# Routing's small products between the last output columns, idle products beside the gather, and gathered rows turned by a diagonal of their scales

## The chip, the cores and the metric

The kernel runs on one core of a Trainium2 chip. The metric is the time of one execution on the device in microseconds; the median of three runs is given with the lowest and the highest. The profile is of one further execution.

## What is computed

Two blocks in a row, in float32, on 512 tokens of 1024 channels. The first block mixes five groups of channels (short convolution, spatial gating, pooling, Conformer convolution, attention to a memory), with a layer norm. The second has two layers, an mLSTM with a SwiGLU and an HGRN2 mixer with a mixture of eight experts, of which each token takes two; a final root-mean-square norm ends it. The change lies in the mixture of experts:

```python
def moe_swiglu(h, router_w, wg, wu, wd):
    t = h.reshape(bsz * s, d)                       # 512 tokens x 1024
    logits = (t @ router_w).astype(jnp.float32)     # 8 experts
    top_logits, top_idx = lax.top_k(logits, TOP_K)  # 2 of 8
    top_w = jax.nn.softmax(top_logits, axis=-1)
    gates = jnp.einsum('tk,tke->te', top_w, jax.nn.one_hot(top_idx, N_EXPERTS))
    for e in range(N_EXPERTS):                      # hidden width 1408
        y = y + gates[:, e:e + 1] * swiglu(t, wg[e], wu[e], wd[e])
```

`h` is `rmsnorm(x) * (1 + scale) + shift`, so an expert's input row is a row of `x` times a scale of its own (the inverse root mean square), times a vector `A` of channels, plus a vector `B` of channels.

## The kernel before, in words

Activations are kept transposed: channels on the 128 partitions, tokens along the free dimension, so `x[0]` to `x[7]` are 128 x 512 each. A product in float32 accuracy is made of three faster ones (`mm3`, `emm`, type fp32r): each operand is split into a high part, copied by ACT, and a low part, the rest, subtracted by DVE. Weights come through `wload` (L238): SP starts a DMA of 128 x 1024 numbers into `raw`, ACT copies `hi`, DVE subtracts `lo`. Small products (routing, rows, bands) are plain float32 ones.

The Tile framework's scheduler sets the order of each engine from priorities that follow the order of the code; `tc.issue_after(i)` puts what stands in its block behind instruction `i`, and `tc.high_priority()` ahead.

**Routing.** The HGRN2 mixer's output projection makes the eight columns of `x`: columns 0 to 3 together (`cols4`), 4 to 7 one by one (`col`, 24 products of 512 columns each). After each, `post(j)` (L1437) adds the residual (`p_h`), and PE makes that column's part of the router logits (`ra`, four products of 8 columns), and of the mean squares (`mean_squares`, after columns 6 and 7). The rows of `x` times `A` also go to DRAM as tokens x channels (`hnd`): `scaled_rows` multiplies four 128 x 128 blocks by diagonals `dg` (tiles named `f` for the first 512 channels and `q` for the last), `to_dram` copies the bank on ACT and starts the DMA. Rows of the first four columns are made after column 3, those of the last four after column 7 and the inverse root `rs`. From the logits DVE ranks the experts (`selb` is the choice), counts the tokens of each and gives each token its place; `dispatch` (one-hot `OH` against `pay`, on PE) turns that into lists of rows `ii` and scales `sc`.

**The rows of an expert.** `fetch` (L1562) has POOL gather an expert's rows from `hnd` by an indirect DMA and then multiplies them by `sc`: for the first expert half on ACT and half on DVE (`now`), for the other seven on POOL (L1573). An expert has places for 192, 128, 192, 128, 160, 128, 160 and 128 rows in the order of the work: a tile of 128 rows, or one of 128 and one of 64 or 32. `inputs` (L1640) turns the rows back into channels x rows: per half of the channels and tile four transposes into one bank, then four ACT copies that add the bias `B` (high part `eh` or `ex`) and four DVE operations for the low part:

```python
nc.tensor.transpose(ps[:, w * k:w * k + w], xg[:, z:z + 128], ident[0:w, 0:w])
pa = act(eh[:, 4 * m + k, o:o + w], ps[:, w * k:w * k + w], AF.Identity, bias=B[:, 4 * m + k:4 * m + k + 1])
pd = stt(el[:, 4 * m + k, o:o + w], ps[:, w * k:w * k + w], B[:, 4 * m + k:4 * m + k + 1],
         eh[:, 4 * m + k, o:o + w].bitcast(F), OP.add, OP.subtract)
```

**An expert** (L1766) makes gate and up products (`hidden_cols` for two tiles, `hidden_rows` for one), then the down products in two halves of 512 channels (`j`), and scatters its rows with addition to `yd` in DRAM by POOL. `then` prepares and fetches the next expert's rows early in the hidden products, and `inputs` of the next expert is written after the first half of the down products. The last expert's rows are added in SBUF (`combine`, L1824), where ACT also squares the sums for the final norm, each column in a scratch buffer of its own, and `final` scales and stores the result. While the first expert starts, ACT's queue also starts the DMAs that prime `yd` (`beside`).

Of the kernel before, what the change touches and what calls it, by code (L numbers as in the profile page):

```python
# [17 lines left out]
T = 512  # L18
NT = 4
# [158 lines left out]
def tile_kernel(ctx, tc, I, out, dbg=None, upto=99):  # L178
# [42 lines left out]
    def mm(o, l, r, start=True, stop=True):  # L221
        nc.tensor.matmul(o, l, r, start=start, stop=stop)  # L222
# [5 lines left out]
    def mm3(o, wh, wl, xh, xl, first, last):  # L228
        mm(o, wh, xh, first, False)
        mm(o, wh, xl, False, False)  # L230
        mm(o, wl, xh, False, last)
# [4 lines left out]
    fast = {"raw": None, "i": 0}  # L236
# [23 lines left out]
    def col(src, xh, xl, post, j, halves=False):  # L260
# [3 lines left out]
        for k0 in range(0, K, 8):  # L264
            m = min(8, K - k0)
            hi, lo = wload(src[:, 128 * k0:128 * (k0 + m)], 128 * m)
            for h in range(2 if halves else 1):
                for r in range(m):
# [4 lines left out]
                    else:  # L273
                        mm3(ps, hi[:, z], lo[:, z], xh[k], xl[k], k == 0, k == K - 1)
# [95 lines left out]
    idle = M(384)  # L370
    for i in range(3):
        mm(idle, O1024, onesk.rearrange("p a b -> p (a b)"))
# [835 lines left out]
    with ExitStack() as st:  # L1208
# [193 lines left out]
        def row_of(v, n, o, bank=M):  # L1402

            ps = bank()
            for k in range(4):
                mm(ps[:, 128 * k:128 * k + 128], v[:, 4 * n + k:4 * n + k + 1].to_broadcast([128, 128]), ident)
            act(o, ps, AF.Copy)

# [14 lines left out]
        def mean_squares(a, last):  # L1423
            for t in range(NT):
                mm(lgm[:, 32 + t:33 + t], ssq[a][:, 128 * t:128 * t + 128], O1024[:, 0:1], False, last and t == 3)
# [10 lines left out]

        def post(j, ps):  # L1437
# [15 lines left out]
        with tc.issue_after(rsqrt(rs[:, 0:4], lgm[:, 32:36], EPS, rs[:, 4:8])):  # L1453
            for t in range(NT):
                to_dram(1, t, scaled_rows(1, t, G()))
# [15 lines left out]
        ts(selb, rk, 2.0, op0=OP.is_lt)  # L1471
# [10 lines left out]
        nc.vector.tensor_copy(out=r8[0], in_=rs[:, None, 0:4].to_broadcast([128, 8, NT]))  # L1482
        parts(pay[..., 2:5], *r8)
# [72 lines left out]

        def tile_of(pays, n0, n, OH, real):
            ps = dispatch(pays, n0, n, OH)
            ii, fi, sc = slots(n, ps, real)
            return n, weights(n, ps), ii, fi, row(n), sc  # L1560

        def fetch(tiles, now=False):  # L1562
# [4 lines left out]
            for t_ in tiles:  # L1567
                r, sc = t_[4], t_[5]
# [24 lines left out]
        fetch(cur, True)  # L1593
# [28 lines left out]
        for n in range(2):  # L1622
            row_of(mods[:, 1, 5, :], n, g2[n], G)
# [5 lines left out]
    with ExitStack() as st:  # L1629
# [10 lines left out]
        def inputs(tiles):  # L1640
# [9 lines left out]
            for m in range(2):  # L1650
                o = 0
                for t_ in tiles:
                    w, xg = t_[0], t_[4]
                    ps = M(4 * w)
                    for k in range(4):
# [9 lines left out]
                pins.append((pa, pd))  # L1665
# [293 lines left out]
```

## Time and profile before

| | us |
|---|---|
| median of three runs (lowest, highest) | 1756.07 (1749.74, 1757.24) |
| profiled execution, its own time | 1755.59 |
| its span in the profile | 1753.8 |
| PE busy | 1702.9 (97%) |
| DVE busy | 1247.8 (71%) |
| ACT busy | 857.6 (49%) |
| POOL busy | 78.1 (4%) |

The profiled execution lasts 1.8 us longer than the span between its first and last recorded work. PE is the engine that is nearly always busy; the mixture of experts runs from about 1201 us, where the last output column ends, to the end. An engine's row in a window gives its busy time, and in brackets the instructions that start there. In a timeline the first number is the start, the second the busy time of the instructions that the row groups (their count stands behind the x); the distance to the next start is what a row of matmuls costs PE, since their ends overlap. What stands in square brackets is idle time ahead of the row and what ended it.

### The profile page before, as it was taken

The page shows a single profiled execution, that of the slowest core. Times are in us where ns is not written, and L with a number is a line of the kernel's source. Part 1 is how long each engine was busy: PE and PEld are TensorE (multiplying, and loading weights), DVE is VectorE, ACT ScalarE, POOL GpSimd, SP SyncE. Part 2 cuts the span into 40 slices and gives each one's busy share as a digit, 9 for nine tenths or more (in the row PEclk, how much of TensorE's full clock was granted, in tenths as well). Part 3 has the DMA queues.
Part 4 walks back from the last instruction along what each step waited for, and adds up shares of the span by engine and source line. Part 5 has one row for each costly group of instructions (what it writes and reads, how often), then busy time and mean ns, then how long its engine had stood idle before and what let it go on. Part 6 is the DMA issues. An engine that isn't in the chain of part 4 may idle for free. (4 is left out here: it accounts for less than half of the span.)

```text
span 1753.8 us, 25198 instructions
## 1 busy us (share of the span) xinstructions
PE 1702.9 (97%) x8987; PEld 1426.5 (81%) x8987; DVE 1247.8 (71%) x2215; ACT 857.6 (49%) x1431; POOL 78.1 (4%) x90
## 2 busy tenths in 40 slices
PE   9999998999999999999999999999999999999995
PEld 7867787787788888888878888787987987978975
DVE  7887888857666766443255766655889889889887
ACT  5535346755443222232243222444667667767675
POOL 1000001000000000000010000000001102011000
PEclk9999998999999999999999999999999999999998
DMA  8434731344426777433342111104879789889885
GB/s 273 138 114 143 228 122 50 108 159 153 154 86 210 241 244 242 140 96 91 105 127 84 58 52 61 61 25 152 311 242 373 248 251 364 266 266 343 263 290 202
DMA packets 96474, 313.02 MB, mean 178 GB/s; under 512 B 10644, under 2 KB 13972, under 8 KB 96344
## 3 DMA queue, kind: packets, MB, share of 16 engines
q1 hardware_dynamic: 90760, 295.88, 50.4%
q0 software_dynamic: 3280, 11.27, 2.8%
q10 hardware_dynamic: 2304, 4.20, 0.6%
q8 instruction: 73, 1.20, 0.3%
q14 instruction: 57, 0.47, 0.1%
HBM read 298.99 MB, written 12.32 MB: 178 GB/s over the span
## 5 line engine op out<-in xcount | busy, mean ns | idle before, releaser
L208 ACT ACTIVATE hi<-raw 128x1024 fp32r<-128x1024 f32 (+3 forms) x473 | 475.5, 1008 | 543.4 <-PE g L222 439.3
L219 DVE TENSOR_TENSOR lo<-raw,hi 128x1024 fp32r<-128x1024 f32 (+3 forms) x473 | 547.7, 1169 | 254.0 <-ACT hi L208 246.0
L222 PE MATMUL g<-xh,hi 128*128 128x512 f32 (+1 forms) x912 | 356.4, 393 | 5.0 <-ACT xh L208 5.0
L222 PE MATMUL g<-xl,hi 128*128 128x512 f32 (+1 forms) x912 | 358.1, 393 | 1.3 <-DVE xl L211 1.2
L222 PE MATMUL g<-xh,lo 128*128 128x512 f32 (+1 forms) x912 | 357.7, 393 | 0.0
L222 PEld LDWEIGHTS g<-xh,hi 128*128 128x128 f32 x912 | 173.5, 191 | 41.5 <-ACT xh L208 5.9
L222 PEld LDWEIGHTS g<-xl,hi 128*128 128x128 f32 x912 | 174.3, 191 | 36.8 <-DVE xl L211 2.8
L222 PEld LDWEIGHTS g<-xh,lo 128*128 128x128 f32 x912 | 174.4, 191 | 33.6 <-issue 1.1
L222 PE MATMUL g<-ex,hi 128*128 128x384 f32 (+1 forms) x704 | 197.1, 359 | 4.3 <-DVE ex L211 4.3
L222 PE MATMUL g<-ex,lo 128*128 128x192 f32 (+1 forms) x704 | 173.7, 247 | 1.7 <-DVE lo L219 1.6
L222 PE MATMUL g<-hi,th 128*128 128x512 f32 (+2 forms) x462 | 148.3, 384 | 0.3 <-ACT th L208 0.2
L388 DVE SCALAR_TENSOR_TENSOR ar<-ar,one,crow 128x1024 f32<-128x1024 f32 x96 | 122.0, 1283 | 24.7 <-DMA ar<-in_ada_dram 22.3
L222 PEld LDWEIGHTS g<-ex,lo 128*128 128x128 f32 x704 | 137.2, 195 | 2.7 <-DVE lo L219 2.6
L222 PEld LDWEIGHTS g<-ex,hi 128*128 128x128 f32 x704 | 135.0, 192 | 5.0 <-DVE ex L211 4.8
L222 PE MATMUL g<-hi,eh 128*128 128x512 f32 (+1 forms) x384 | 112.9, 373 | 0.0
L222 PE MATMUL g<-lo,th 128*128 128x512 f32 (+2 forms) x275 | 104.9, 382 | 0.0
L222 PEld LDWEIGHTS g<-hi,th 128*128 128x128 f32 (+1 forms) x462 | 83.1, 183 | 19.7 <-ACT th L208 1.3
L222 PEld LDWEIGHTS g<-hi,eh 128*128 128x128 f32 x384 | 70.8, 188 | 10.1
L222 PE MATMUL g<-lo,eh 128*128 128x512 f32 (+1 forms) x192 | 71.8, 374 | 4.0 <-DVE lo L219 4.0
L222 PE MATMUL g<-fh,hi 128*128 128x512 f32 (+1 forms) x198 | 73.1, 369 | 0.0
L222 PE MATMUL g<-fl,hi 128*128 128x512 f32 (+1 forms) x198 | 72.7, 367 | 0.0
L222 PE MATMUL g<-fh,lo 128*128 128x512 f32 (+1 forms) x198 | 72.7, 367 | 0.0
(473 smaller groups left out, 2516.3 us busy)
## 6 DMA issues: line engine op xcount, KB each, us to landing
ar<-in_ada_dram SPq DMA_DIRECT2D x96, 512.0 KB, 4.4
raw<-in_e_w_dram SPq DMA_DIRECT2D x88, 512.0 KB, 5.1
raw<-in_e_d_dram SPq DMA_DIRECT2D x79, 512.0 KB, 4.9
raw<-in_e_a_dram SPq DMA_DIRECT2D x64, 512.0 KB, 4.7
raw<-in_f_gu_dram SPq DMA_DIRECT2D x44, 512.0 KB, 3.6
raw<-in_e_b_dram SPq DMA_DIRECT2D x32, 384.0 KB, 7.5
raw<-in_w_in_dram SPq DMA_DIRECT2D x22, 512.0 KB, 3.5
raw<-in_f_d_dram SPq DMA_DIRECT2D x16, 512.0 KB, 3.5
```

The lines of the kernel that those rows point to most:

```text
L208: return nc.scalar.activation(out=o, in_=i, func=f, **kw).ins
L219: return nc.vector.tensor_tensor(out=o, in0=a, in1=b, op=op).ins
L222: nc.tensor.matmul(o, l, r, start=start, stop=stop)
L388: nc.vector.scalar_tensor_tensor(out=raw, in0=raw, scalar=pace["one"], in1=crow, op0=OP.mult, op1=OP.mult, accum_out=mods[:, l, i, j:j + 1])
```

## The change

Five things are changed.

1. Logits and rows of finished columns are issued behind later columns: after column 4 the logits of columns 0 and 1 and the first half's rows of token blocks 0 and 1, after column 5 those of 2 and 3, after column 6 the logits of 4, 5 and 6 and the row products of columns 4 and 5 (`later_rows`), which stay in four banks; those of columns 6 and 7 come after the last logits and the last mean squares.
2. The parts of `rs` for the payload (`r8`) are issued after the choice.
3. Four idle float32 products of 384 columns follow the products of `g2`, beside the gather.
4. Gathered rows are no longer multiplied by their scales. DVE makes a diagonal of an expert's scales (`diagonal`), and `inputs` multiplies: one float32 product of the identity with `B`, spread over the bank, and per block of channels the rows with the diagonal, added to it. One ACT copy and one DVE subtraction follow per half and tile. `inputs` is now a generator, of which a piece is issued after each weight load of the second down half.
5. All squares of `combine` use one scratch buffer (`l4`).

```diff
+        def logits(j):
+            for t in range(NT):
+                i = mm(lgm[:, 8 * t:8 * t + 8], x[j][:, 128 * t:128 * t + 128], ra[:, 8 * j:8 * j + 8], False, False)
+            return i
+        def later_rows(k):
+            if not late_rows:
+                late_rows.extend([M(), M(), M(), G()])
+            for t in range(NT):
+                mm(late_rows[t][:, 128 * k:128 * k + 128], x[4 + k][:, 128 * t:128 * t + 128], dg[4 + k])
         def post(j, ps):
             p_h(j, ps)
-            for t in range(NT):
-                mm(lgm[:, 8 * t:8 * t + 8], x[j][:, 128 * t:128 * t + 128], ra[:, 8 * j:8 * j + 8], False, False)
+            at = fast["mm"]
+            with tc.issue_after(at):
+                for i in {4: (0, 1), 5: (2, 3), 6: (4, 5, 6)}.get(j, ()):
+                    logits(i)
+            for t in {4: (0, 1), 5: (2, 3)}.get(j, ()):
+                with tc.issue_after(at):
+                    ps = scaled_rows(0, t, M())
+                to_dram(0, t, ps)
             if j == 6:
                 mean_squares("a", False)
+                with tc.issue_after(at):
+                    later_rows(0)
+                    later_rows(1)
             if j == 7:
-                mean_squares("b", True)
-            if j == 3:
-                for t in range(NT):
-                    to_dram(0, t, scaled_rows(0, t, M()))
+                with tc.issue_after(logits(7)):
+                    later_rows(2)
+                with tc.issue_after(mean_squares("b", True)):
+                    later_rows(3)
...
+        def diagonal(n0, n, sc):
...
+                diag["t"] = hp.tile([128, T], F, tag=("l5", "l6")[diag["i"]], name="dgs")
+            d = diag["t"][0:n, n0:n0 + n]
+            ts(d, ident[0:n, 0:n], sc[:, 0:1])
+            return d
...
-                if now:
-                    act(r[:, 0:512], r[:, 0:512], AF.Copy, scale=sc[:, 0:1])
-                    ts(r[:, 512:1024], r[:, 512:1024], sc[:, 0:1])
-                else:
-                    nc.gpsimd.tensor_tensor(out=r, in0=r, in1=sc[:, 0:1].to_broadcast([t_[0], D]), op=OP.mult)
...
-            row_of(mods[:, 1, 5, :], n, g2[n], G)
+            i = row_of(mods[:, 1, 5, :], n, g2[n], G)
+        idle_mms(4, i)
...
+                    mm(p3, ident, B[:, ks, None].to_broadcast([128, 4, w]), True, False)
                     for k in range(4):
                         z = 512 * m + 128 * k
-                        nc.tensor.transpose(ps[:, w * k:w * k + w], xg[:, z:z + 128], ident[0:w, 0:w])
-                    for k in range(4):
-                        pa = act(eh[:, 4 * m + k, o:o + w], ps[:, w * k:w * k + w], AF.Identity,
-                                 bias=B[:, 4 * m + k:4 * m + k + 1])
-                    for k in range(4):
-                        pd = stt(el[:, 4 * m + k, o:o + w], ps[:, w * k:w * k + w], B[:, 4 * m + k:4 * m + k + 1],
-                                 eh[:, 4 * m + k, o:o + w].bitcast(F), OP.add, OP.subtract)
+                        mm(p3[:, k], xg[:, z:z + 128], d, False, k == 3)
+                    pa = act(eh[:, ks, o:o + w], p3, AF.Copy)
+                    pd = tt(el[:, ks, o:o + w], p3, eh[:, ks, o:o + w].bitcast(F), OP.subtract)
...
                     hi, lo = wload(src, w * kn)
+                    if j == 1 and ahead is not None:
+                        xn_ = next(ahead, xn_)
...
-                act(hw(f"l{4 + j}")[:, 0:w], a, AF.Square, accum=fz[:, j, t:t + 1])
+                act(hw("l4")[:, 0:w], a, AF.Square, accum=fz[:, j, t:t + 1])
```

How the order of instructions moves, at three places. First, PE behind column 6, whose last product is the first row (`x_1841` to `x_1843` are the columns 4 to 6, `ra` logits, `q` row products, `onesk` mean squares, `yh` and `yl` the parts of column 7's operand):

```order
 L222 MATMUL g<-yh_7468,lo 128x512
+L222 MATMUL m<-ra,x_1841 128x8 x4
+L222 MATMUL m<-ra,x_1842 128x8 x4
+L222 MATMUL m<-q,x_1841 128x128 x3
+L222 MATMUL g<-q,x_1841 128x128
+L222 MATMUL m<-ra,x_1843 128x8 x4
+L222 MATMUL m<-q,x_1842 128x128 x3
+L222 MATMUL g<-q,x_1842 128x128
 L222 MATMUL g<-yh_7461,hi 128x512
+L222 MATMUL m<-onesk,ssq 128x1 x4
 L222 MATMUL g<-yl_7469,hi 128x512
 L222 MATMUL g<-yh_7461,lo 128x512
```

Twelve products of logits and eight of rows now stand between columns 6 and 7. Before, those logits stood inside columns 5, 6 and 7, the four mean squares in the middle of column 7, and the row products behind it.

Second, PE at the end of the first expert's down products, where a one-tile expert's rows are turned (`row` gathered rows, `dgs` the diagonal, `mods` the bias, `cst` the identity, `th` the hidden activations). Before:

```order
L222 MATMUL g<-hi,th 128x512 x2
L222 MATMUL g<-lo,th 128x512
L1657 MATMUL m<-cst,row 128x128 x8
L222 MATMUL g<-hi,th 128x512
L222 MATMUL g<-lo,th 128x512
```

and now:

```order
L222 MATMUL m<-mods,cst 128x512
L222 MATMUL m<-dgs,row 128x128 x4
L222 MATMUL g<-hi,th 128x512
L222 MATMUL g<-lo,th 128x512
L222 MATMUL g<-hi,th 128x512 x2
L222 MATMUL g<-lo,th 128x512
L222 MATMUL g<-hi,th 128x512
L222 MATMUL g<-lo,th 128x512
L222 MATMUL g<-hi,th 128x512 x2
L222 MATMUL g<-lo,th 128x512
L222 MATMUL m<-mods,cst 128x512
L222 MATMUL m<-dgs,row 128x128 x4
```

The eight transposes in one place become ten products in two places, five to each, with down products between.

Third, DVE before a two-tile expert begins (`ex` its inputs' low part, `lo` low parts of weights, `row` the expert's rows that are scattered). Before:

```order
L211 SCALAR_TENSOR_TENSOR ex<-m,mods,ex 128x64 x3
L211 SCALAR_TENSOR_TENSOR ex<-m,mods,ex 128x128
L219 TENSOR_TENSOR lo<-raw,hi 128x1024
L211 SCALAR_TENSOR_TENSOR ex<-m,mods,ex 128x128
L219 TENSOR_TENSOR lo<-raw,hi 128x1024 x3
L211 SCALAR_TENSOR_TENSOR ex<-m,mods,ex 128x128 x2
L211 SCALAR_TENSOR_TENSOR ex<-m,mods,ex 128x64 x4
L211 SCALAR_TENSOR_TENSOR row<-g,iw,g_9863 128x512
L211 SCALAR_TENSOR_TENSOR row<-g,iw,g_9864 128x512
```

and now:

```order
L219 TENSOR_TENSOR ex<-m,ex 128x4x128
L219 TENSOR_TENSOR lo<-raw,hi 128x1024
L219 TENSOR_TENSOR ex<-m,ex 128x4x64
L219 TENSOR_TENSOR lo<-raw,hi 128x512
L219 TENSOR_TENSOR ex<-m,ex 128x4x128
L219 TENSOR_TENSOR lo<-raw,hi 128x1024
L219 TENSOR_TENSOR ex<-m,ex 128x4x64
L219 TENSOR_TENSOR lo<-raw,hi 128x1024
L211 SCALAR_TENSOR_TENSOR row<-g,iw,g_9863 128x512
L219 TENSOR_TENSOR lo<-raw,hi 128x1024 x2
```

The last seven small operations stood behind the weights' subtractions and directly ahead of the rows; now the fourth and last `ex` has three weights' subtractions and a row behind it before the next expert's own work.

## Rows read from the trace of the kernel before

**Rows 1.** The page, part 1: busy time, share of the span, instructions of each engine.

```profile
PE 1702.9 (97%) x8987; PEld 1426.5 (81%) x8987; DVE 1247.8 (71%) x2215; ACT 857.6 (49%) x1431; POOL 78.1 (4%) x90
```

**Rows 2.** Windows: us, busy of PE, PEld, DVE, ACT, POOL (count), clock, DMA share, GB/s.

```profile
1201.09:1221.61 20.52, 17.16 (x146) 14.75 (x145) 15.41 (x82) 12.69 (x29) 2.08 (x2) 0.93 0.58 178
1221.61:1246.00 24.39, 22.67 (x146) 21.67 (x145) 18.70 (x43) 17.01 (x34) 3.95 (x2) 0.92 1.02 397
1246.00:1715.00 469.00, 459.79 (x2649) 407.42 (x2649) 408.72 (x647) 329.66 (x533) 50.84 (x29) 0.99 0.87 289
1488.30:1491.70 3.40, 3.40 (x16) 3.40 (x16) 3.40 (x13) 2.57 (x5) 2.53 (x2) 0.50 0.88 240
1715.00:1753.80 38.80, 21.08 (x128) 18.41 (x127) 27.02 (x47) 19.53 (x47) 0.00 (x0) 0.79 0.52 182
1218.64:1225.47 6.83, 6.21 (x30) 5.25 (x31) 4.97 (x18) 5.64 (x19) 0.00 (x0) 0.50 1.01 387
```

**Rows 3.** Timeline, transposes of a 128-row tile: start, busy us, engine, line, op, count.

```profile
1288.56 1.03 PE L1657 MATMUL m<-cst,row 128*128 128x128 f32 x8
1289.35 0.48 PE L222 MATMUL g<-hi,th 128*128 128x512 f32 x1
```

**Rows 4.** PE's timeline, float32 products of 512 and of 128 columns, and what follows.

```profile
1134.09 1.02 PE L222 MATMUL g<-k,onesk 128*128 128x512 f32 x2
1134.94 0.49 PE L1338 MATMUL m<-cst,k 128*128 128x128 f32 x3
1204.36 2.25 PE L222 MATMUL g<-q,x 128*128 128x128 f32 x18
1206.45 0.60 PE L1619 MATMUL g<-cst,x 128*128 128x128 f32 x4
```

**Rows 5.** PE's timeline, float32 products of eight columns, and what follows them.

```profile
1202.20 0.96 PE L222 MATMUL m<-ra,x 128*128 128x8 f32 x8
1203.02 0.69 PE L222 MATMUL g<-q,x 128*128 128x128 f32 x4
```

**Rows 6.** PE's waits from 1246 to 1715 (total, times, longest), then PE's timeline.

```profile
PE g L222 <- DVE ex L211: 4.3, 3, 1.5
PE g L222 <- DVE lo L219: 4.0, 3, 1.3
PE m L1759 <- DVE eh L219: 0.8, 3, 0.3
...
1331.17 0.35 PE L222 MATMUL g<-lo,eh 128*128 128x384 f32 x1
1331.35 0.52 PE L222 MATMUL g<-hi,eh 128*128 128x384 f32 x2
1333.19 0.44 PE L222 MATMUL g<-lo,eh 128*128 128x384 f32 x1 [1.32 <-DVE lo L219]
1486.85 0.41 PE L222 MATMUL g<-ex,hi 128*128 128x320 f32 x1 [1.51 <-DVE ex L211]
```

**Rows 7.** Timeline, POOL and DVE: scaling of rows, one DVE operation beside it and alone.

```profile
1322.85 0.27 DVE L215 TENSOR_SCALAR OH<-cst,P1r 128x128 bf16<-128x128 f32 x1
1329.91 2.27 POOL L1573 TENSOR_TENSOR row<-row,sc 64x1024 f32<-64x1024 f32 x1 [0.30 <-DMA row<-hnd,ii]
1330.36 1.91 DVE L215 TENSOR_SCALAR OH<-cst,P1r 128x128 bf16<-128x128 f32 x1
```

**Rows 8.** PE's timeline after column 3: the last row products and the next column.

```profile
1171.46 4.25 PE L222 MATMUL m<-f,x 128*128 128x128 f32 x24
1175.47 0.47 PE L222 MATMUL g<-yh,hi 128*128 128x512 f32 x1
```

**Rows 9.** Timeline, first expert: ACT on the second gather's rows, PE's longest wait.

```profile
1218.40 0.72 ACT L208 ACTIVATE row<-row,sc 64x512 f32<-64x512 f32 x1 [0.77 <-DMA row<-hnd,ii]
1242.01 0.36 PE L222 MATMUL g<-ex,lo 128*128 128x192 f32 x1 [1.25 <-DVE lo L219]
```

**Rows 10.** PE's timeline of the tail, the records that wait longest.

```profile
1736.94 1.66 PE L222 MATMUL m<-el,eh 128*128 128x256 f32 x8 [2.29 <-ACT el L208]
```

More of the change, by code (lines that the diff above doesn't have):

```diff
@@ L221, in mm, with idle_mms @@
     def mm(o, l, r, start=True, stop=True):
-        nc.tensor.matmul(o, l, r, start=start, stop=stop)
+        return nc.tensor.matmul(o, l, r, start=start, stop=stop).ins
+    def idle_mms(n, after=None):
+        with ExitStack() as order:
+            if after is not None:
+                order.enter_context(tc.issue_after(after))
+            ps = M(384)
+            for i in range(n):
+                mm(ps, O1024, onesk.rearrange("p a b -> p (a b)"))
     def split(hi, lo, src):
@@ L230, in mm3 @@
         mm(o, wh, xl, False, False)
-        mm(o, wl, xh, False, last)
+        return mm(o, wl, xh, False, last)
     def log_exp_tables():
         return tc.keep_in_program_order(nc.scalar.preload_act_table_set("natural_log_exp_and_others")).ins
-    fast = {"raw": None, "i": 0}
+    fast = {"raw": None, "i": 0, "mm": None}
     def wload(src, n, after=()):
@@ L368, in tile_kernel @@
     O256, O1024, O128 = onesk[:, 0, :], onesk[:, 1, :], onesk[:, 2, :]
-    idle = M(384)
-    for i in range(3):
-        mm(idle, O1024, onesk.rearrange("p a b -> p (a b)"))
+    idle_mms(3)
     pairsel = const.tile([8, 4, 128], F, name="pairsel")
@@ L1424, in mean_squares @@
             for t in range(NT):
-                mm(lgm[:, 32 + t:33 + t], ssq[a][:, 128 * t:128 * t + 128], O1024[:, 0:1], False, last and t == 3)
+                i = mm(lgm[:, 32 + t:33 + t], ssq[a][:, 128 * t:128 * t + 128], O1024[:, 0:1], False, last and t == 3)
+            return i
         def scaled_rows(n, t, ps):
@@ L1454, in tile_kernel @@
             for t in range(NT):
-                to_dram(1, t, scaled_rows(1, t, G()))
+                to_dram(1, t, late_rows[t])
         L = SM("L", 32)
@@ L1470, in tile_kernel @@
         nc.vector.reduce_sum(out=rk.rearrange("p (t e) -> p t e", e=8), in_=c4, axis=AX.X)
-        ts(selb, rk, 2.0, op0=OP.is_lt)
+        chosen = ts(selb, rk, 2.0, op0=OP.is_lt)
         ts(sel, rk, 2.0, op0=OP.is_lt)
@@ L1481, in tile_kernel @@
         r8 = [lp.tile([128, 8, NT], F, name=f"r8{i}") for i in range(2)]
-        nc.vector.tensor_copy(out=r8[0], in_=rs[:, None, 0:4].to_broadcast([128, 8, NT]))
-        parts(pay[..., 2:5], *r8)
+        with tc.issue_after(chosen):
+            nc.vector.tensor_copy(out=r8[0], in_=rs[:, None, 0:4].to_broadcast([128, 8, NT]))
+            parts(pay[..., 2:5], *r8)
         pp, pc = M(32), M(8)
@@ L1555, in weights @@
             return iw
+        diag = {"i": 0}
+        def diagonal(n0, n, sc):
+            if n0 == 0:
+                diag["i"] = 1 - diag["i"]
+                diag["t"] = hp.tile([128, T], F, tag=("l5", "l6")[diag["i"]], name="dgs")
+            d = diag["t"][0:n, n0:n0 + n]
+            ts(d, ident[0:n, 0:n], sc[:, 0:1])
+            return d
         def tile_of(pays, n0, n, OH, real):
@@ L1559, in tile_of, with fetch @@
             ii, fi, sc = slots(n, ps, real)
-            return n, weights(n, ps), ii, fi, row(n), sc
-        def fetch(tiles, now=False):
+            return n, weights(n, ps), ii, fi, row(n), diagonal(n0, n, sc)
+        def fetch(tiles):
             for t_ in tiles:
@@ L1592, in tile_kernel @@
             cur.append([n, None, ii, fi, row(n), sc])
-        fetch(cur, True)
+        fetch(cur)
+        for c, n0 in zip(cur, (0, 128)):
+            c[5] = diagonal(n0, c[0], c[5])
         with tc.issue_after(last[0]):
@@ L1769, in expert @@
             else:
-                xs, pins = inputs(tiles)
+                xs, pins = list(inputs(tiles))[-1]
             ns = [t_[0] for t_ in tiles]
-            after = []
+            after, ahead, xn_ = [], None, None
             def then():
@@ L1800, in expert @@
                 if j == 0 and after:
-                    after.append(inputs(after[0]))
+                    ahead = inputs(after[0])
                 for i, n in enumerate(ns):
@@ L1816, in expert @@
                         in_=yts[i], in_offset=None, compute_op=OP.add)
+            if after:
+                after.append(xn_)
             return after
@@ L1932, in tile_kernel @@
             x_ = [tile_of(xpay, 0, 128, places(xP, 128), True)]
-            fetch(x_, True)
+            fetch(x_)
             expert(e, x_, combine)
```

22 lines of the change are left out of this document (14 added, 8 removed).

## The prediction

> **What bounds it now.** I read the page's busy shares first. TensorE (PE) is busy 97% of the span, VectorE (DVE) 71%, ScalarE (ACT) 49% and GpSimd (POOL) 4% [rows 1]. So a microsecond that the change adds to PE's work is paid in full unless PE waited there anyway, and one that it takes off POOL or ACT pays only where PE waited for them. The windows then divide the part that the change touches [rows 2]. In the routing (1201.09 to 1221.61) PE works 17.16 of 20.52 us, and part of that is filler. In the first expert's start (1221.61 to 1246.00) it works 22.67 of 24.39 us while the DMA share is 1.02. In the seven further experts (1246 to 1715) it works 459.79 of 469.00 us at a granted clock of 0.99: all that can be won there is 9.2 us of waiting and the spells at 1.2 GHz. The tail (1715 to 1753.80) is 21.08 us of PE in 38.80.
>
> **Turning the rows, after the first expert.** Now eight transposes turn a 128-row tile, and PE gives them 0.79 us (1288.56 to 1289.35) [rows 3]; I charge a narrow tile the same. The change takes them out and puts in, for each half of a tile, one float32 product that spreads the bias over the bank and four that multiply 128 columns of rows by the diagonal. Every float32 product of the trace leaves two records. Two records of 512 columns took 0.85 us from one start to the next; eighteen records of 128 columns took 2.09 us (1204.36 to 1206.45), 0.116 each [rows 4]; narrow ones took 0.103 (0.82 for eight) [rows 5]. For 256 and 128 columns of bias I scale 0.85 to 0.43 and 0.21.
> - A one-tile expert: 2 x (0.85 + 8 x 0.116) = 3.56 less 0.79, +2.8. Four of them: +11.1.
> - A tile of 128 and one of 64: 2 x (0.85 + 0.43 + 0.93 + 0.82) = 6.06 less 1.58, +4.5. One such expert after the first.
> - A tile of 128 and one of 32: 2 x (0.85 + 0.21 + 0.93 + 0.82) = 5.62 less 1.58, +4.0. Two: +8.1.
>
> Together **+23.7 us**, all on PE, which has no room for it: it sits in the stream of the second down half, a piece per weight load. The lower end is the transposes' own spacing, 0.098 per record: 112 records of 128 columns would cost 2.0 less. The upper end is the price taken: the q products have the same shape and ran back to back. The Trainium skill ("TensorE: Matmul & The Clock Gate", Back-to-back issue gap) gives about 81 ns per matmul of 128 columns in a sustained stream; worked out from that page, an estimate, those 112 records would cost 3.9 us less. Row 1204.36 disagrees and decides.
>
> **What goes away there.** The waits of PE that the trace lists are 4.3 us for the last low parts of the next expert's inputs (three times, up to 1.5) and 4.0 us for low halves of weights (three times, up to 1.3) [rows 6]. With a third row they make 9.1 us, nine waits. Each hides some 0.17 us more in the record ahead of it: the two products at 1331.35 and the one at 1333.19 start 1.84 us apart, where two such products take 0.35 (starts at 1331.17 and 1331.35 are 0.18 apart), so 1.49 is lost and 1.32 booked. That makes 10.6 us. The causes:
> - A POOL multiplication of rows by their scales runs 2.27 us, and a DVE operation beside it that takes 0.27 elsewhere took 1.91 [rows 7]. The weights' subtraction behind it came late, and it is the one that 1333.19 waits for; I read the other two waits for weights as of the same kind. All ten POOL multiplications go.
> - At a two-tile handover DVE makes 16 small subtractions, and PE waits at the first product of the next expert. Now one per half and tile, four in all, stand among the weights' subtractions: in DVE's new order the last is followed by a weights' subtraction, a row and two more before anything of the next expert.
>
> After two of these three waits the clock fell: behind the one at 1486.85 it was 0.50 from 1488.30 to 1491.70 [rows 2, 6], and a second spell of 3.4 us like it makes up the 0.99 of the stretch (3.4 x 0.5 x 2 is 0.7% of 469). Half of 3.4 us, twice: 3.4. In all **-14.0 us**. The ends: nothing comes back of the 4.5 us and 3.4 (rival D), or all of it does.
>
> What is late next: PE's own stream. The new ACT copies (one for four) and DVE subtractions are fewer and lie beside it. The ten diagonals on DVE are each one tensor-scalar operation of 128 columns like the 0.27 row, some 2.7 us in all, spread over seven experts with DVE at 408.72 of 469 us: I cost them at nothing; without that cover each is 0.27.
>
> **Routing's small products.** The rows of the first four columns and their logits stood as one cluster after column 3; its last 24 records of 128 columns took 4.01 us (1171.46 to 1175.47), 0.167 each against 0.116, since the clock was low there [rows 8]. Divided among columns 4 and 5, they cost 1.2 us less if it holds. Against this, sixteen q records now run between columns 6 and 7 that before filled PE's time behind column 7, +1.9. The end of column 7 comes about 0.6 later; if the new cluster behind column 6 made a spell of its own, 1.7 more. After it the mean squares stand behind eight records of rows, not four: +0.46. The parts of the scales, issued after the choice, take work out of DVE's chain ahead of the gather that nobody there waits for; I take nothing, 0.3 either way.
>
> **The first expert's inputs.** ACT and DVE scale the rows of the second gather at 1218.40, as they land, and the first product starts at 1221.61, 3.21 us behind [rows 2, 9]. Without the scaling, PE owes after that landing the narrow tile's first four products and both tiles' second half, 0.82 + (0.85 + 0.93) + (0.43 + 0.82) = 3.85 us at 2.4 GHz (+0.6), or twice that at 1.2 GHz (+4.5). The clock was at 0.50 from 1218.64 to 1225.47 [rows 2], after PE had waited; the products from 1221.61 on lost half of 3.86 us by it, 1.9. So the ends are -1.3 (the four idle products hold the clock) and +4.5 (they don't). I take 0.0: they cover the wait for the first landing, not that for the second. The idle products themselves run in that wait; without it they would cost 4 x 0.64 us, 384 columns at the 512-column price. POOL's multiplication in this stage goes too, and with it most of the 1.25 us that PE waited at 1242.01 [rows 9]: -1.1. Stage: 0.6 + 0.46 + 0.0 - 1.1 = **0.0**, from -2.4 to +4.
>
> **The tail.** Records of the last column's sums wait 2.29 us for a part that ACT splits behind squares of the column before [rows 10]. With one scratch buffer for all squares ACT's order changes and that part stands ahead of the second column's squares; DVE's last row operations remain. I take **-0.8**, between -1.5 and +1 (a square that waits for its buffer).
>
> **Sum:** +23.7 - 14.0 + 0.0 - 0.8 = +8.9 on the profiled execution's 1755.59, so **1764.5**. The median of the runs is 0.48 above that execution, less than the sum is good for, and I leave it out. Half a per cent, 8.8 us, is what a measurement of this kernel can tell from no change: the forecast lies on that line.
>
> **Rivals.**
> - **B, cheaper products and a held clock, 1759.** Records at 0.098 (-2.0), the first stage at its best (-2.4), the tail at its best (-0.7). For it: each end has a row. Against: the q records.
> - **C, one pass, 1745 (the other side).** If a float32 product against a diagonal or the identity took one record like the transposes, a one-tile expert would add 2 x (0.43 + 4 x 0.098) - 0.79 = +0.85, the 192 one +1.24, the 160 ones +1.06: +6.8 for +23.7. That gives 1747.6, and with B's stage and tail 1744.5. It decides from one record per product. For it: the transposes, whose data are float32 too, have one. Against: the bands of q and k are plain float32 products and have two each.
> - **D, the handovers stay late, 1772.** The subtractions are fewer, but each now needs a bias product and four more on PE first, and the pieces come one per weight load. If the last DVE subtraction of a two-tile handover ends after PE's last down product, the three waits (4.5 us) and the spells (3.4) remain: 1764.5 + 7.9 = 1772.4. For it: three of three such handovers waited. Against: the new order of DVE. On the spells the rows say that they come after the waits: a granted clock of 0.99 over seven handovers with transposes [rows 2] leaves room for the two seen. The Trainium skill (same page, Part 4: PE-mode transpose) says that transposes don't count as work for the clock in the same way; by it products would hold the clock whatever the waits do, and D would be 3.4 less, 1769. The five handovers with transposes and no spell speak against that, so it gets 0.03 of D's chance.
> - That the change doesn't do what it says: by the orders above every moved part goes where the code asks for it, so no chance is kept for that.
>
> **Chances.** Forecast 0.45, B 0.20, C 0.12, D 0.23. The forecast's own range is 1759 to 1770, half of it on each side of the line: same 0.22, slower 0.23. B: same 0.19, faster 0.01. C: faster 0.10, same 0.02. D: slower. Sums: faster 0.11, same 0.43, slower 0.46. The range of 1749 to 1774 leaves out most of C (0.11) and the top of D (0.05).
>
> **What would show it.** Right: two records per turning product, 0.85 us for the widest bias product and 0.93 for four of the diagonal's; PE busy in 1246 to 1715's counterpart some 20 us more; no POOL multiplication; no wait for ex at a first product and no clock of 0.50 there; the stage from column 7 to the first product about as long as now. Wrong: one record per product (C), ex waits of over a microsecond (D), a spell behind column 6 or through the first turning (up to +6), or a down half in which PE waits for the weights that the pieces delay, which no row shows.

## The result and the profile after

The changed kernel takes 1766.15 us (median of 8 runs, 1762.65 to 1772.56), the kernel before, on the same chip, 1753.92 (8 runs, 1748.59 to 1757.24): a ratio of 1.0075 with a 95% interval of 1.0061 to 1.0088. It is slower by more than half a per cent; the forecast was 1764.5, on the line. Part of that nearness is luck: the forecast stood on 1755.59, 1.7 us above the 1753.92 here, and its difference was +8.9 where the medians are 12.2 apart. The profiled execution took 1767.26 us.

Part 1 of the page of the changed kernel, against [rows 1]:

```profile
PE 1724.8 (98%) x9139; PEld 1442.5 (82%) x9139; DVE 1228.2 (70%) x2153; ACT 846.4 (48%) x1357; POOL 62.5 (4%) x80
```

PE gained 21.9 us of work and the span 11.7; DVE, ACT and POOL all lost some. The windows by stage, with the columns of [rows 2]: the last output columns, the routing, the first expert's hidden products, the seven further experts, the tail.

```profile
1138.17:1201.90 63.73, 63.73 (x341) 52.94 (x340) 29.37 (x45) 25.02 (x41) 0.00 (x0) 1.00 0.07 26
1201.90:1226.72 24.82, 22.70 (x157) 18.74 (x156) 16.74 (x79) 12.18 (x23) 2.00 (x2) 0.93 0.61 209
1226.72:1277.08 50.36, 50.36 (x359) 50.29 (x358) 41.28 (x80) 35.47 (x66) 0.95 (x1) 1.00 0.89 312
1277.08:1727.21 450.13, 448.89 (x2558) 391.23 (x2557) 365.56 (x548) 300.61 (x432) 33.80 (x20) 1.00 0.85 285
1727.21:1765.50 38.29, 21.37 (x127) 18.14 (x126) 26.74 (x47) 19.59 (x47) 0.00 (x0) 0.82 0.51 179
```

The same stages of the kernel before, where [rows 2] cut them otherwise (the routing stands there):

```profile
1137.42:1201.09 63.67, 63.67 (x325) 52.64 (x324) 29.38 (x45) 25.02 (x41) 0.00 (x0) 0.97 0.07 25
1221.61:1276.06 54.45, 52.73 (x358) 51.73 (x356) 44.54 (x90) 38.11 (x74) 3.95 (x2) 0.96 0.90 316
1276.06:1715.17 439.11, 429.90 (x2438) 377.53 (x2437) 383.05 (x599) 308.73 (x492) 50.84 (x29) 0.99 0.87 292
1715.17:1753.80 38.63, 20.91 (x127) 18.24 (x126) 26.86 (x47) 19.36 (x47) 0.00 (x0) 0.79 0.52 181
```

The clock was granted in full from the first expert on until the tail, where before it was 0.96 and 0.99, and in the further experts PE now waits 1.2 us in place of 9.2. The starts of the first product of each stage on PE's timeline give the account by stage (us of the profiled executions; a stage lasts until the next one's first product):

| stage | before | after | difference | forecast |
|---|---|---|---|---|
| all ahead of the output projection, which the change leaves alone | 1137.42 | 1138.17 | +0.75 | |
| projection and routing, to the first expert's first product | 84.19 | 88.55 | +4.36 | |
| first expert's hidden products | 54.45 | 50.36 | -4.09 | 0.0 with the row above |
| down products with the turning of one tile (4) | 104.02 | 114.64 | +10.62 | +11.1 |
| down products with the turning of two tiles (3) | 54.40 | 68.18 | +13.78 | +12.6 |
| hidden products of the seven further experts | 280.69 | 267.31 | -13.38 | -14.0 |
| last down products and tail | 38.63 | 38.29 | -0.34 | -0.8 |

The turning of the second half of a two-tile expert's inputs, on PE's timeline, against [rows 3, 4, 5]:

```profile
1352.98 1.02 PE L222 MATMUL m<-mods,cst 128*128 128x512 f32 x2
1353.84 1.05 PE L222 MATMUL m<-dgs,row 128*128 128x128 f32 x8
1354.64 0.48 PE L222 MATMUL g<-hi,th 128*128 128x512 f32 x1
...
1356.12 0.59 PE L222 MATMUL m<-mods,cst 128*128 128x256 f32 x2
1356.65 1.10 PE L222 MATMUL m<-dgs,row 64*128 64x64 f32 x8
1357.68 0.50 PE L222 MATMUL g<-hi,th 128*128 128x512 f32 x1
```

Each product leaves two records. The bias takes 0.86 us (1352.98 to 1353.84), the wide tile's four products 0.80 (to 1354.64); the narrow tile's five take 0.53 and 1.03 (1356.12 to 1357.68). That is 3.22 us for this half of both tiles, eight blocks, where eight transposes of a 128-row tile took 0.79.

What PE waits for from the first expert's first product to the end of the last hidden ones, against [rows 6], is one line:

```profile
PE m L1804 <- DVE eh L219: 1.2, 2, 1.0
```

The waits for `ex` and `lo` are gone. The diagonals cost DVE what was taken for them:

```profile
1325.51 0.28 DVE L215 TENSOR_SCALAR dgs<-cst,sc 128x128 f32<-128x128 f32 x1
```

Before the first expert PE runs without a pause from the products of `g2` through the idle products (`onesk`), the weights' dispatch and the first bias product:

```profile
1214.25 2.83 PE L222 MATMUL g<-cst,mods 128*128 128x128 f32 x16
1216.92 2.75 PE L222 MATMUL m<-onesk 128*128 128x384 f32 x8
1219.50 0.46 PE L222 MATMUL m<-pay,OH 128*128 128x3 bf16 x8
1219.89 1.13 PE L222 MATMUL m<-mods,cst 128*128 128x512 f32 x2
```

The idle products take 2.58 us (1216.92 to 1219.50), all four bias products of the turning stand behind them, and the first product of the expert starts only at 1226.72. Behind column 6 the small products now run at full clock: six records of row products from 1192.76 to 1193.51, 0.125 each, against the 0.167 of [rows 8]:

```profile
1192.76 0.91 PE L222 MATMUL m<-q,x 128*128 128x128 f32 x6
1193.51 0.39 PE L222 MATMUL g<-q,x 128*128 128x128 f32 x2
1193.73 0.96 PE L222 MATMUL m<-ra,x 128*128 128x8 f32 x8
```

In the tail of this execution, PE's longest wait for ACT's part is shorter than the 2.29 us of [rows 10]:

```profile
PE m L222 <- ACT el L208: 0.5, 1, 0.5
```

### The profile page after: what moved, and what is told of

Read it like the earlier page. It is cut to its first block, busy times and chain, and to the rows that moved or that the text cites. A ratio compares the mean times of both kernels' runs of the same rounds, so it can differ in the third digit from the quotient of the medians.

```text
span 1765.5 us, 25317 instructions
## 1 busy us (share of the span) xinstructions
PE 1724.8 (98%) x9139; PEld 1442.5 (82%) x9139; DVE 1228.2 (70%) x2153; ACT 846.4 (48%) x1357; POOL 62.5 (4%) x80
## 5 line engine op out<-in xcount | busy, mean ns | idle before, releaser
L222 PE MATMUL g<-ex,hi 128*128 128x384 f32 (+1 forms) x704 | 191.3, 352 | 0.0
```

Of the source, the lines that this page charges most:

```text
L222: return nc.tensor.matmul(o, l, r, start=start, stop=stop).ins
```

## The experiments

Each kernel was timed against the kernel before, in five rounds. A ratio's interval of 0.2 to 0.5% is 3 to 8 us, so small effects are read from the profiles, as the time from the output projection's first product to the end (616.4 us before, 627.3 after): the part ahead of it differs by itself from run to run (last section). The stage of further experts is 1277 to 1727 us in the changed kernel. My theory: the turning on PE makes the loss, and the waits that went paid half of it back. The rival: the moved small products and the idle ones make it, since the first product of the first expert came 4.4 us later.

**Routing alone.** The kernel before with changes 1, 2, 3 and 5; rows scaled and transposed as before.

```diff
+            at = fast["mm"]
+            with tc.issue_after(at):
+                for i in {4: (0, 1), 5: (2, 3), 6: (4, 5, 6)}.get(j, ()):
+                    logits(i)
...
+        idle_mms(4, i)
```

> The kernel before with the routing's small products moved, the parts of the scales behind the choice, the idle products and the one scratch buffer for the squares, but rows scaled and transposed as before. My theory (the turning on PE makes the loss): the first product of the first expert comes 0 to 2 us later, the clock holds in the first expert's start (up to 3 us back), the tail gives 0.4; in all -1 +- 2 against the kernel before, and the waits for ex and lo at the handovers stay (some 8 us in the stretch of the seven further experts). Rival (the moved products and the idle ones make the loss, since the first product came 4.4 us later in the changed kernel): +4 or more.

Measured: ratio 1.0001 (0.9986 to 1.0017), 615.3 us from the projection on. PE's waits in the experts:

```profile
PE g L222 <- DVE ex L211: 4.3, 3, 1.5
PE g L222 <- DVE lo L219: 4.1, 3, 1.4
```

They are those of [rows 6]. These parts of the change make neither loss nor gain, and do not touch the handovers: the rival falls. The clock did not hold as expected, though: it was 0.97 over the first expert's hidden products, with the idle products in place.

**Turning alone.** The kernel before with change 4 only.

```diff
+                    mm(p3, ident, B[:, ks, None].to_broadcast([128, 4, w]), True, False)
                     for k in range(4):
                         z = 512 * m + 128 * k
-                        nc.tensor.transpose(ps[:, w * k:w * k + w], xg[:, z:z + 128], ident[0:w, 0:w])
+                        mm(p3[:, k], xg[:, z:z + 128], d, False, k == 3)
```

> The kernel before with the turning by diagonals alone: no scaling of rows, float32 products for the turning, one copy and one subtraction per half and tile. My theory: +24.4 of PE in the seven further experts less 13.4 of waits and clock, +3 before the first product (6.8 us of turning for 4.2), -1.6 of weight waits behind it: +12 to +13 against the kernel before, no wait for ex and none for lo over 1 us in that stretch. Rival (the moved products make the loss): +5 or less.

Measured: ratio 1.0065 (1.0042 to 1.0088), 11.4 us; 625.3 us from the projection on, +8.9. PE's waits in the experts:

```profile
PE m L1769 <- DVE eh L219: 1.8, 2, 1.0
PE g L222 <- DVE lo L219: 0.4, 1, 0.4
```

This is the loss. The +3 before the first product did not come: from the projection to that product it took 84.3 us, as before (84.2). Two of the four bias products ran before the rows had landed (at 1204.29 and 1207.86). And without any idle products the first expert's hidden products ran at full clock:

```profile
1216.76:1267.47 50.71, 50.71 (x359) 50.63 (x358) 41.69 (x81) 35.58 (x66) 0.95 (x1) 1.00 0.89 318
```

**Without the idle products.**

```diff
-        idle_mms(4, i)
```

> The changed kernel without its four idle products. My theory: their 2.6 us stand on the path, since PE goes from the products of g2 through them straight to the turning without a wait: -1 to -2.5 against the changed kernel if the clock holds, about 0 if a spell at half clock (1.7 us) follows the wait for the gather. Rival (the idle products hold the clock through the turning and the first weights): +2 or more, with a granted clock of 0.50 over the turning.

Measured: ratio 1.0075 (1.0052 to 1.0098), that of the changed kernel. The first product came 2.4 us earlier behind the projection (86.1 us for 88.55), as the theory has it. Then PE waited for an input, and a spell (a stretch at half clock) lay not over the turning but over the first weights:

```profile
1227.33 0.69 PE L222 MATMUL g<-ex,hi 128*128 128x384 f32 x1 [1.38 <-DVE ex L219]
1227.00:1233.00 6.00, 5.67 (x21) 5.67 (x22) 4.12 (x5) 2.33 (x3) 0.00 (x0) 0.50 1.04 414
```

and the first expert's hidden products took 54.9 us for 50.4. The idle products cost what they take, and in this order what they keep away is worth as much by the ratios and 2 us more by the stages of these two executions. The theory's second case (about 0, with a spell) comes nearest, but the spell lasted from 1226.82 to 1233.65, and half of that is 3.4 us, not its 1.7. The second experiment had the full clock without the idle products, so not every order needs them.

**Rows scaled by ACT, turned by transposes.** From the changed kernel: rows of the seven further experts are multiplied by their scales in one operation of ACT each, transposed; ACT adds the bias in four operations into a scratch buffer, then one copy and one subtraction.

```diff
+                    act(t_[4], t_[4], AF.Copy, scale=t_[5][:, 0:1])
...
-                        mm(p3[:, k], xg[:, z:z + 128], d, False, k == 3)
+                        nc.tensor.transpose(p3[:, k], xg[:, z:z + 128], ident[0:w, 0:w])
+                    for k in range(4):
+                        act(f[:, k], p3[:, k], AF.Identity, bias=B[:, 4 * m + k:4 * m + k + 1])
-                    pa = act(eh[:, ks, o:o + w], p3, AF.Copy)
-                    pd = tt(el[:, ks, o:o + w], p3, eh[:, ks, o:o + w].bitcast(F), OP.subtract)
+                    pa = act(eh[:, ks, o:o + w], f, AF.Copy)
+                    pd = tt(el[:, ks, o:o + w], f, eh[:, ks, o:o + w].bitcast(F), OP.subtract)
```

> The changed kernel with the rows turned by transposes again, scaled by ACT at the handover (128 x 1024 in one operation; the first expert's rows by ACT and DVE as before), the bias added by ACT in four operations into a scratch buffer, then one copy and one subtraction per half and tile; nothing on POOL but gathers and scatters. My theory: the 24.4 us of PE go and the waits stay away, since POOL and DVE are as free as in the changed kernel: -24 to -28 against it, some 1740, 14 us below the kernel before. Rival (four small operations of ACT per half put the last inputs late again, with waits for ex of 1.3 to 1.5 us and spells): -16 or less, 1748 to 1750.

Measured: ratio 1.0081 (1.0058 to 1.0105). Both missed by 15 us and more. The timeline of ACT and PE at the first of three such places:

```profile
1325.91 1.15 ACT L208 ACTIVATE row<-row,sc 128x1024 f32<-128x1024 f32 x1 [4.47 <-DMA row<-hnd,ii]
1329.44 1.11 PE L1804 MATMUL m<-cst,eh 128*128 128x128 f32 x4 [4.40 <-DVE eh L219]
```

The scheduler had put the scaling early in ACT's queue, where it stood 4.47 us for the gather; weight copies queued behind it, and PE waited 4.40 us for DVE. A wait put on an engine that feeds others costs what stands behind it.

**Bias back on ACT and DVE.** The changed kernel without the bias product; four small operations of ACT and four of DVE per half and tile, as before. POOL stays idle.

```diff
-                    mm(p3, ident, B[:, ks, None].to_broadcast([128, 4, w]), True, False)
...
+                    for k in range(4):
+                        pd = stt(el[:, 4 * m + k, o:o + w], p3[:, k], B[:, 4 * m + k:4 * m + k + 1],
+                                 eh[:, 4 * m + k, o:o + w].bitcast(F), OP.add, OP.subtract)
```

> The changed kernel without the float32 product of the bias: the products with the diagonal alone turn the rows, and the bias is added by four operations of ACT and four of DVE per half and tile, as in the kernel before; nothing on POOL. My theory (each bias product costs 0.85 us per 512 columns on PE): 13.7 us less in the seven further experts and up to 2.6 before the first product, so -14 to -16 against the changed kernel; whether the waits for ex (4.3 us and up to two spells of 1.7) come back tells whether the small operations or POOL made them: if they do, -7 to -10.

Measured: ratio 1.0017 (1.0002 to 1.0033), some 10 us less than the changed kernel. The down products with a one-tile turning took 107.8 us for 114.6: 6.9 less, and by the 0.85 that was expected for each product, two to a tile, 4 x 1.70 should go. PE's waits in the experts:

```profile
PE g L222 <- DVE ex L211: 4.2, 4, 1.4
PE g L222 <- DVE lo L219: 1.6, 2, 0.9
```

The waits for `ex` are back with POOL idle: the many small operations make them. It is not that PE comes to the inputs sooner: at the last handover DVE's last `ex` ends 7.6 us behind the last turning product, where it is 1.3 us in the changed kernel. Those for `lo` are two short ones.

**POOL adds zero.** The changed kernel with one POOL operation, which changes nothing, on each gathered tile of the seven further experts.

```diff
+            for t_ in tiles if pool else ():
+                nc.gpsimd.tensor_tensor(out=t_[4], in0=t_[4], in1=zcol[0:t_[0], 0:1].to_broadcast([t_[0], D]), op=OP.add)
```

> The changed kernel with one operation of POOL added on each gathered tile of the seven further experts, which adds zero to the rows where the kernel before multiplied them by their scales. My theory (POOL's operation holds DVE up): the waits for lo come back, some 4 us in the seven further experts, and the wait behind the first expert's start too: +3 to +6 against the changed kernel, a DVE operation of over 1.5 us beside each POOL operation, no wait for ex. Rival (the many small DVE operations made the weights late): within 1.

Measured: ratio 1.0095 (1.0080 to 1.0110), 3.5 us above the changed kernel by the ratios, whose intervals just overlap, and 9.2 by the profiles. POOL and DVE, and later PE's longest wait, on the timeline:

```profile
1334.27 1.89 POOL L1613 TENSOR_TENSOR row<-row,zcol 128x1024 f32<-128x1024 f32 x1 [7.06 <-DMA row<-hnd,ii]
1334.36 3.48 DVE L219 TENSOR_TENSOR lo<-raw,hi 128x768 fp32r<-128x768 f32 x2
...
1349.57 0.52 PE L1806 MATMUL m<-cst,eh 128*128 128x128 f32 x3 [3.96 <-DVE eh L219]
```

and DVE's same two subtractions in the changed kernel:

```profile
1329.84 1.81 DVE L219 TENSOR_TENSOR lo<-raw,hi 128x768 fp32r<-128x768 f32 x2
```

Two that take 1.81 us took 3.48 beside POOL's 1.89. The time went to PE not as waits for `lo` (0.6 us) but for hidden activations (4.8 us in all) that stood behind late weights on DVE. There was no wait for `ex`. So POOL's operation holds DVE up, as argued, and what waits for it changes with the queue.

**ACT's scaling issued later.** As the fourth experiment, the scaling issued on ACT behind the last weight copy of the first down half.

```diff
+                        order.enter_context(tc.issue_after(scale))
...
+                    ahead = inputs(after[0], fast["act"])
```

> As the fourth experiment, but the scaling of the rows is issued on ACT behind the last weight copy of the first down half, so that ACT waits for no gather. My theory: 24.4 us of PE go, the 13 us of waits of the fourth experiment too: -22 to -27 against the changed kernel, 1740 to 1744. Rival (four operations of ACT per half put the inputs late): waits for ex of 1.3 us at three handovers, -16 to -19.

Measured: ratio 0.9977 (0.9964 to 0.9989), 17 us below the changed kernel and 4 below the one before. The rival's number came, with its waits:

```profile
PE g L222 <- DVE ex L219: 5.0, 5, 1.7
PE m L1807 <- DVE eh L219: 2.6, 3, 1.0
```

**Scaled on the way out.** ACT's copies of the rows take the inverse root, and four more scale the first four columns' rows in place before their DMA.

```diff
-            act(h, ps, AF.Copy)
+            if n == 0 and ps is not None:
+                act(h, ps, AF.Copy)
+                return
+            act(h, h if ps is None else ps, AF.Copy, scale=rs[:, t:t + 1])
```

> Rows are scaled by the inverse root on their way to DRAM instead (ACT's copies of the last four columns' rows take the scale, and four more of ACT scale the first four columns' rows in place before their DMA), so that no gathered row is scaled at all; turned by transposes, bias by ACT. My theory: no scaling at any handover and none before the first transposes: -24 to -29 against the changed kernel, 1737 to 1742. Rival (four more operations of ACT and later DMAs stand ahead of the gather): the first product comes 1 to 3 us later, -21 to -24.

Measured: ratio 1.0032 (1.0018 to 1.0045), 7.5 us below the changed kernel. From the first product on it is 17 us faster than that, but the product came at 97.3 us behind the projection's start, not 88.55:

```profile
1212.03 1.06 ACT L208 ACTIVATE hi<-raw 128x1024 fp32r<-128x1024 f32 x1 [4.09 <-DMA raw<-in_e_w_dram]
1215.48 2.18 PE L1651 MATMUL g<-cst,x 128*128 128x128 f32 x9 [6.62 <-ACT xrow L208]
```

A weight copy stood ahead of the last two scalings on ACT and waited 4.09 us for its DMA; the copies that free PE's banks stood behind both, and PE 6.62 us behind those.

**The same, in order.** The first weight copy is issued behind the rows' DMAs, and the turning begins at the third weight load of the first down half.

```diff
+                    behind = ((out_last,) if beside is not None else ()) if pins is None or not u else pins[min(u, 2) - 1]
...
+                    if nl_ >= 3 and after:
+                        with tc.issue_after(mark):
+                            xn_ = next(ahead, xn_)
```

> As the eighth experiment, with its two delays taken away: the first weight copy of the first expert is issued on ACT behind the DMAs of the rows, and the turning starts from the third weight load of the first down half on, each piece behind the product before it on PE. My theory: the 6.6 us that PE waited for ACT in the routing go and the first product comes as early as in the changed kernel or up to 2 us earlier; in the further experts the waits for ex shrink from 3.3: -17 to -22 against the changed kernel, 1744 to 1749, 5 to 9 below the kernel before. Rival (the rows' DMAs, later by four copies of ACT, hold the gather): -12 to -15.

Measured: ratio 1.0007 (0.9994 to 1.0020), 12 us below the changed kernel. The rival's number, not for its reason: the weight copy now stands behind the scalings, and still ahead of the copies for PE.

```profile
1213.71 1.06 ACT L208 ACTIVATE hi<-raw 128x1024 fp32r<-128x1024 f32 x1 [2.93 <-DMA raw<-in_e_w_dram]
1215.43 2.82 PE L1651 MATMUL g<-cst,x 128*128 128x128 f32 x12 [5.73 <-ACT xrow L208]
```

**ACT's scaling, early.** As the seventh experiment, with the scaling behind the second weight load of the first down half and the turning from the fourth on.

```diff
+                    if nl_ == 2 and after:
+                        ahead = inputs(after[0], fast["act"])
+                        next(ahead)
+                    if nl_ >= 4 and ahead is not None:
+                        with tc.issue_after(mark):
+                            xn_ = next(ahead, xn_)
```

> As the seventh experiment (rows scaled by ACT at the handover, turned by transposes, bias by ACT), with the scaling behind the second weight load of the first down half and the turning from the fourth load on, each piece behind the product before it on PE. My theory: the seventh experiment lost to its waits for ex (5.0 us, five of them), which come from pieces that start too late; they go to 2 or less and the rest stays: -17 to -20 against the changed kernel, 1746 to 1749. Rival (DVE's queue, not the start of the pieces, makes the last input late): waits for ex as before, 1749 to 1752.

Measured: 1746.33 us, ratio 0.9962 (0.9945 to 0.9978): 20 below the changed kernel, 7 below the one before, the lowest median of all (the seventh's interval overlaps). The size is the theory's, the waits are not:

```profile
PE g L222 <- DVE ex L219: 4.0, 3, 1.5
PE m L1808 <- DVE eh L219: 1.7, 1, 1.7
```

Three waits for `ex` stay at the three two-tile handovers. At the last of them the chain reads:

```profile
1592.62 0.43 PE L1701 MATMUL m<-cst,row 32*128 32x32 f32 x4
1602.84 0.31 ACT L208 ACTIVATE ex<-el 128x128 fp32r<-128x128 f32 x1
1603.90 0.29 DVE L219 TENSOR_TENSOR ex<-el,ex 128x128 fp32r<-128x128 f32 x1
```

The last transposes start at 1592.62, ACT's copy of their result only 10.2 us later, behind weight copies and small additions in its queue; DVE follows after 1.1. So neither text had the cause: the pieces start early enough, and ACT's queue, not DVE's, makes the last input late. What went is in the down products with two tiles, 54.5 us for the seventh experiment's 58.8. PE also still waits 2.28 us directly ahead of the first expert's first product (1222.39), which no run pursued.

## Why the prediction was right, step by step

**Turning, +23.7: +24.4 by the stages.** Two records per product, so the case of one pass (C) falls. Eight records of 128 columns took 0.80 us, 0.100 each, for the 0.116 of [rows 4]; the one-tile experts came out 0.5 lower for it. The Trainium skill ("TensorE: Matmul & The Clock Gate", Back-to-back issue gap), with 81 ns, points the right way and is below what this trace shows for float32. The narrow tile's products took 1.03 for 0.82 and its bias 0.53 for 0.43, which gave that back. The trace's single records show that the three prices of the forecast (0.116, 0.103, 0.098) are nearly one: within a run, records of float32 products start 0.111 us apart, from 1353.84 with 128 columns, from 1356.65 with 64 (its first two 0.16) and in the logits of [rows 5] with 8, and the transposes of [rows 3] 0.109. What differs is the way to the neighbours, 0.03 us from the last record to the next product behind the wide tile and 0.20 behind the narrow one. The two-tile experts are 1.2 higher than forecast. 0.4 of that are PE's small waits there for DVE, 0.8 us in the third line of [rows 6] and 1.2 now, in the line for L1804 above; the step that failed counted them among those that go. The other 0.8 was not traced.

**What goes away, -14.0: -13.4.** (The three waits of rival D are 4.3 us by [rows 6], 4.8 with their hidden parts, not its 4.5.) The two causes were separated: POOL's operation makes weights and activations late (sixth experiment), the many small operations make the inputs late (fifth). The spells went with the waits. The handovers staying late (D) did not happen; but the fifth, seventh and tenth experiments have the waits for `ex` of over a microsecond and no half clock at the handovers of the further experts, so a wait does not by itself bring a spell, and what brings one stays open. Nor do transposes, which the seventh and tenth have: the rule of the Trainium skill (same page, Part 4: PE-mode transpose) shows no effect there. At the first expert the runs leave it open: over its hidden products the seven kernels that transpose were granted 0.94 to 0.97, and of the five that multiply four had 1.00 (the third experiment 0.94); but in the seven PE also waits, for 0.6 to 2.3 us, at the last transposes or right behind them.

**First stage, 0.0: +0.3, by terms that were off and cancelled, which is luck.** The sign that this stage up to the first product would last about as long as before did not come: 24.8 us for 20.5. Column 7's end was to come 0.6 later; the window of the last output columns grew by 0.06, since the divided clusters ran at a clock of 1.00 where one cluster had 0.97. The step that failed is "the idle products themselves run in that wait": PE came to them without a wait and paid 2.6 us, as their removal shows; the turning stood behind them, so that PE still owed 6.4 us when the second rows had landed (1220.34), not 3.85. In the second experiment, without them, it was 4.4 (1212.32 to 1216.76). The full clock of the first weights and the `lo` waits that went gave back 4.1 us. Of the range, -2.4 left out two of the stage's own terms (0.6 and 0.46); with them it is -1.3.

**Tail, -0.8: -0.3, and not by its mechanism.** The wait for ACT's part is 1.8 us shorter in the changed kernel's execution. The step that failed is that one scratch buffer brings this: the first and the third experiment have the one buffer, and ACT still runs that part behind three squares of 256 columns, as before; PE waited 2.5 us and, in the third,

```profile
PE m L222 <- ACT el L208: 2.4, 1, 2.4
```

What set ACT's order otherwise in the changed kernel stays open.

**The sum**, +8.9, against 11.7 in the profiles (0.75 of them ahead of the change) and 13 by the ratio. The stages differ from the forecast by 2.1 us: 1.2 of two tiles, 0.6 of the waits, 0.5 of the tail and 0.3 of the first stage, less 0.5 of one tile. PE's work in the further experts rose from 429.9 to 448.9 us, close to the 20 that was to show it. What is left between profiles and ratio is within what runs of one kernel differ by; it was not settled.

## What to carry to other kernels

On an engine that is busy all the time, price the work that is moved to it at its own rows before counting the waits that go: here 24 us of products bought 13 us of waits. Most of that could be had without the products (8.5 of the 13.4 us in the tenth experiment's hidden products): scale on an engine with time (ACT) and keep the transposes, but name the place in its queue, since the same operation issued too early made the kernel 18 us slower. Where an idle engine's work slows a busy neighbour, as POOL did DVE, take it off that engine first.

## What was not expected of the hardware

The part of the program ahead of the output projection, the same instructions in all twelve kernels, lasted from 1130.68 us (seventh experiment) to 1138.91 (sixth) in their profiled executions. These 8 us are more than most effects here, so stages were compared from a mark behind it. The granted clock goes with them; the two parts (sixth, seventh), with PE's clock third from the end:

```profile
0.00:1138.91 1138.91, 1118.70 (x5606) 911.42 (x5607) 747.74 (x1358) 453.73 (x750) 25.37 (x57) 0.99 0.42 136
0.00:1130.68 1130.68, 1109.54 (x5606) 903.98 (x5607) 747.28 (x1358) 453.23 (x750) 20.30 (x57) 1.00 0.42 137
```

The seventh had no spell there, the sixth six of 3.4 us each at 0.50, which would cost a PE that is always busy 10 us. The twelve stand in the order of their spells: one 1131.4 and 1132.5 us, two 1134.1, three 1134.3, five 1134.9, six 1135.6 to 1138.9. What brings a spell in one execution and not in the next stays open.

And two weights' subtractions on DVE took 3.48 us beside one POOL addition of 1.89 us, not 1.81: one operation of an engine that is 4% busy held its neighbour up for nearly its whole length.
